# A 3x3 convolution with residual: the weights' load moved to third place on SyncE's queue, and other waits and semaphores for the loads

## The chip, the cores and the metric

The kernel runs on one core of a Trainium2 chip. The metric is the device time of one execution in microseconds (us); for the kernel before it is the median of three runs. A profile is one more execution, recorded by the hardware profiler, with its own span and time.

## The reference

Sixteen images with 64 channels of 64 x 64 pixels are convolved with a 3 x 3 kernel (64 channels out, zero padding of 1), and a residual is added, all in fp32:

```python
x:        (16, 64, 64, 64)      # batch, c_in, h, w
weight:   (64, 64, 3, 3)        # c_out, c_in, kh, kw
residual: (16, 64, 64, 64)
output[b, co] += weight[co, ci, kh, kw] * x_pad[b, ci, kh:kh+h, kw:kw+w]   # over ci, kh, kw
return output + residual
```

## The kernel before, in words

**Data and tiles.** Two images make a pair: 2 x 64 channels on 128 partitions, 4096 pixels each, 2 MB of fp32. There are eight pairs. Pair p of x is loaded into `xr[p % 3]`, one of three buffers. Its residual is loaded into `ro[p]`, one of eight; the sum is written in place there, and `ro[p]` is stored. So every pair costs three transfers of 2 MB. The weights (64 x 576 fp32, 144 KB) are loaded into `wdup`, which lies inside the last residual buffer, `ro[7]`.

**ScalarE** issues the weights' load (L125) and then packs the images. For each image n two copies (L135, L136) cast the even and the odd rows of x to bf16 and put them on the two halves of the partitions of `xp[n % 4]`. The first copy of a pair waits for the pair's load (`s_x`, L132), and from image 4 on each image waits until the convolution that last read its `xp` buffer is done (`s_conv`, L134).

**TensorE** first transposes the weights (L174), nine small matmuls into PSUM, as soon as DVE has doubled them (L145). Then it runs 16 convolutions of 24 matmuls each (L82 loads new weights first, L83 doesn't). Before an image it waits for a free PSUM half (`s_bank`, L178) and for the packed image (`s_pack`, L179). At the end of an image it raises `s_conv`. The result goes to `ps[n % 2]`, one of two halves of PSUM.

**DVE** clears the borders, waits for the weights (`s_w`, L144), doubles them (L145), casts the transposed weights to the bf16 tile `wl` (L152), and then adds the residual: for each image two adds (L163), for the even and the odd rows. It waits for the pair's residual (`s_r`, L160) and for the convolution (`s_conv`, L161). The first add of an image raises `s_add`, the second one frees the PSUM half (`s_bank`); of the last image both raise `s_add`.

**SyncE** issues all other transfers, in an order written out by hand: x0, r0, x1, r1, x2, r2, then for p = 3 to 7 a wait for the convolution of both images of pair p - 3 (L102), because pair p takes its x buffer, followed by x and r of that pair. The last residual also waits until the weights in its buffer have been transposed (`s_wt`). Then come the stores of pairs 0 to 4, each of which waits for `s_add` at 2p + 3 (L108), the first add of the next pair. The last three stores (L197) stand outside the critical section: they are issued when all engines have come to its end.

```python
        for p in range(NPAIR):
            if p >= NXR:
                nc.sync.wait_ge(s_conv, 2 * (p - NXR) + 2)
            load_x(p)
            if p == NPAIR - 1:
                nc.sync.wait_ge(s_wt, 2)
            load_ro(p)
        for p in range(NEARLY):
            nc.sync.wait_ge(s_add, 2 * p + 3)
            store(p).then_inc(s_out, 16)
```

Of the kernel before, what the change touches and what calls it, by code (L numbers as in the profile page):

```python
# [13 lines left out]
@with_exitstack  # L14
def kernel(
    ctx: ExitStack,
    tc: tile.TileContext,
    x: bass.AP,
    weight: bass.AP,
    residual: bass.AP,  # L20
    out: bass.AP,
):
    nc = tc.nc

    B, C, H, W = x.shape
    CO = weight.shape[0]
    K = weight.shape[2]
    assert C == 64 and CO == 64 and K == 3 and H == 64 and W == 64 and B == 16

    NPIX = H * W  # L30
    NPAIR = B // 2
    J = H // 2
    JC = 8
    NCHUNK = J // JC
    NXR = 3
    NXP = 4
    NEARLY = 5

    res_bc = residual.rearrange("b c h w -> (b c) (h w)")
    out_bc = out.rearrange("b c h w -> (b c) (h w)")  # L40
    x_bc = x.rearrange("b c h w -> (b c) (h w)")
    w_flat = weight.rearrange("co ci kh kw -> co (ci kh kw)")

    pool = ctx.enter_context(tc.tile_pool(name="pool", bufs=1))
    psum = ctx.enter_context(tc.tile_pool(name="psum", bufs=1, space=bass.MemoryType.PSUM))

    ident = pool.tile([64, 64], FP32)
    ro = [pool.tile([128, NPIX], FP32, name=f"ro{p}") for p in range(NPAIR)]
    xr = [pool.tile([128, NPIX], FP32, name=f"xr{i}") for i in range(NXR)]

    xp = [pool.tile([128, J + 1, W], BF16, name=f"xp{i}") for i in range(NXP)]

    wdup = ro[NPAIR - 1][0:64, 0:1152].rearrange("p (d f) -> p d f", d=2)
    wl = pool.tile([128, 2, 3, 2, 64], BF16)
    ps = [psum.tile([128, NCHUNK, JC, W], FP32, name=f"ps{i}") for i in range(2)]

    sem = lambda name: tc.alloc_semaphore(name)
    s_w = sem("s_w")
    s_x = [sem(f"s_x{p}") for p in range(NPAIR)]
    s_r = [sem(f"s_r{p}") for p in range(NPAIR)]  # L60
    s_out = sem("s_out")
    s_id = sem("s_id")
    s_wt = sem("s_wt")
    s_pack = sem("s_pack")
    s_bank = sem("s_bank")
    s_conv = sem("s_conv")
    s_add = sem("s_add")

    def load_x(p):
        nc.sync.dma_start(out=xr[p % NXR][:, :], in_=x_bc[128 * p : 128 * p + 128, :]).then_inc(s_x[p], 16)  # L70

    def load_ro(p):
        nc.sync.dma_start(out=ro[p][:, :], in_=res_bc[128 * p : 128 * p + 128, :]).then_inc(s_r[p], 16)

    def store(p):
        return nc.sync.dma_start(out=out_bc[128 * p : 128 * p + 128, :], in_=ro[p][:, :])

    def matmul(out_, lhsT, rhs, start, stop, ldweights):

        e = nc.tensor  # L80
        if ldweights:
            return e.matmul(out=out_, lhsT=lhsT, rhs=rhs, start=start, stop=stop, skip_group_check=True)  # L82
        return e.add_instruction(  # L83
            mybir.InstMatmult(
                name=nc.get_next_instruction_name(),
                engine=PE,
                ins=[e.lower_ap(rhs), e.lower_ap(lhsT)],
                outs=[e.lower_ap(out_)],
                start_tensor_calc=start,
                stop_tensor_calc=stop,  # L90
                tile_size=(128, 128),
                tile_position=(0, 0),
                bass_skip_group_check=True,
                ldweights=False,
            )
        )

    with tc.tile_critical(no_gpsimd_drain=True):  # L98

        for p in range(NPAIR):  # L100
            if p >= NXR:
                nc.sync.wait_ge(s_conv, 2 * (p - NXR) + 2)  # L102
            load_x(p)
            if p == NPAIR - 1:
                nc.sync.wait_ge(s_wt, 2)
            load_ro(p)
        for p in range(NEARLY):
            nc.sync.wait_ge(s_add, 2 * p + 3)  # L108
            store(p).then_inc(s_out, 16)


        nc.gpsimd.memset(ident[:, :], 0.0).then_inc(s_id, 1)  # L112
        nc.gpsimd.wait_ge(s_id, 1)
        nc.gpsimd.affine_select(  # L114
            out=ident[:, :],
            in_=ident[:, :],
            compare_op=mybir.AluOpType.not_equal,
            fill=1.0,
            base=0,
            pattern=[[-1, 64]],  # L120
            channel_multiplier=1,
        ).then_inc(s_id, 1)


        nc.scalar.dma_start(out=wdup[:, 0, :], in_=w_flat[:, :]).then_inc(s_w, 16)  # L125
        for n in range(B):
            p, im = divmod(n, 2)
            hp = slice(64 * im, 64 * im + 64)
            x4 = xr[p % NXR].rearrange("q (j two w) -> q j two w", two=2, w=W)
            t = xp[n % NXP]  # L130
            if im == 0:
                nc.scalar.wait_ge(s_x[p], 16)  # L132
            if n >= NXP:
                nc.scalar.wait_ge(s_conv, n - NXP + 1)  # L134
            nc.scalar.copy(out=t[64:128, 0:J, :], in_=x4[hp, :, 0, :])  # L135
            nc.scalar.copy(out=t[0:64, 1 : J + 1, :], in_=x4[hp, :, 1, :]).then_inc(s_pack, 1)  # L136


        for t in xp:
            nc.vector.memset(t[0:64, 0, :], 0.0)  # L140
            nc.vector.memset(t[64:128, J, :], 0.0)  # L141
        nc.vector.memset(wl[0:64, 0, :, 1, :], 0.0)  # L142
        nc.vector.memset(wl[64:128, 1, :, 0, :], 0.0)  # L143
        nc.vector.wait_ge(s_w, 16)  # L144
        nc.vector.tensor_copy(out=wdup[:, 1, :], in_=wdup[:, 0, :]).then_inc(s_wt, 1)  # L145
        nc.vector.wait_ge(s_wt, 2)
        tpf = ps[0].rearrange("p c j w -> p (c j) w")

        blocks = ((0, 0, 0, 0), (1, 0, 0, 1), (1, 0, 1, 0), (0, 1, 0, 2), (0, 1, 1, 1), (1, 1, 1, 2))
        for half, d, par, kh in blocks:  # L150
            hp = slice(64 * half, 64 * half + 64)
            i = nc.vector.tensor_copy(out=wl[hp, d, :, par, :], in_=tpf[hp, 3 * kh : 3 * kh + 3, :])  # L152
        i.then_inc(s_bank, 2)
        for n in range(B):
            p, im = divmod(n, 2)
            hp = slice(64 * im, 64 * im + 64)
            o4 = ro[p].rearrange("q (j two w) -> q j two w", two=2, w=W)
            psj = ps[n % 2].rearrange("q c j w -> q (c j) w")
            if im == 0:
                nc.vector.wait_ge(s_r[p], 16)  # L160
            nc.vector.wait_ge(s_conv, n + 1)  # L161
            for par in range(2):
                i = nc.vector.tensor_tensor(  # L163
                    out=o4[hp, :, par, :], in0=psj[64 * par : 64 * par + 64, :, :], in1=o4[hp, :, par, :], op=ADD
                )

                i.then_inc(s_add if par == 0 or n == B - 1 else s_bank, 1)


        nc.tensor.wait_ge(s_id, 2)  # L170
        nc.tensor.wait_ge(s_wt, 1)
        wdup3 = wdup.rearrange("p d (ci t) -> p (d ci) t", t=9)
        for t in range(9):
            i = nc.tensor.transpose(out=ps[0][:, t // 8, t % 8, :], in_=wdup3[:, :, t], identity=ident[:, :])  # L174
        i.then_inc(s_wt, 1)
        with nc.Fori(0, B // NXP, 1, engines=[PE]):
            for n in range(NXP):
                nc.tensor.wait_ge(s_bank, 1).then_inc(s_bank, -1)  # L178
                nc.tensor.wait_ge(s_pack, 1).then_inc(s_pack, -1)  # L179
                order = [(1, 0), (1, 1), (0, 0), (0, 1), (2, 0), (2, 1)]  # L180
                for i, (kw, d) in enumerate(order):
                    xlo, xhi = max(0, 1 - kw), min(W, W + 1 - kw)
                    for c in range(NCHUNK):
                        j0 = JC * c
                        m = matmul(
                            ps[n % 2][:, c, :, xlo:xhi],
                            wl[:, d, kw, :, :].rearrange("q r c -> q (r c)"),
                            xp[n][:, j0 + d : j0 + d + JC, xlo + kw - 1 : xhi + kw - 1],
                            i == 0,
                            i == len(order) - 1,  # L190
                            c == 0,
                        )
                m.then_inc(s_conv, 1)


    for p in range(NEARLY, NPAIR):
        store(p)  # L197
    with tc.tile_critical(sync_engine=mybir.EngineType.Pool, no_gpsimd_drain=True):
        nc.gpsimd.wait_ge(s_out, 16 * NEARLY)
# [30 lines left out]
```

## Time and profile before

| what | value |
|---|---|
| median of 3 runs | 124.96 us (124.82 to 125.03) |
| the profiled execution: its time | 125.16 us |
| the profiled execution: its span | 123.3 us |
| moved by DMA | 50.48 MB, mean 409 GB/s |
| TensorE matmuls, busy | 85.9 us (70% of the span) |
| VectorE (DVE), busy | 76.6 us (62%) |
| ScalarE (ACT), busy | 62.0 us (50%) |
| the adds, L163 | 32 of 2289 ns |
| the packing copies, L135 and L136 | 32 of about 1.9 us |

The span runs from the first to the last event that the profile shows of the program; the time is 1.9 us longer. Names in the profile: PE is TensorE's matmuls, PEld its weight loads, SP is SyncE, and SPq or ACTq is the queue of instructions on which SyncE or ScalarE issues transfers. In a row of the timeline stand the start and the duration in us, the engine, the line, the operation with the tile that it writes and the tile that it reads, and in brackets how long the engine had been idle and what ended that. A row of windows has the stretch, its length, the busy time of PE, PEld, DVE, ACT and POOL, PE's granted clock, the mean busy share of the 16 DMA engines and the GB/s. A row of waits has the total, the number of waits and the longest one. The weights are part of the buffer `ro`, and are shown under that name.

### The profile page before, as it was taken

The numbers are of one execution on the slowest core, as the hardware profiler recorded it, in microseconds if no ns is written. First come the engines' busy times: TensorE is split into PE (matmuls) and PEld (weight loads), VectorE is DVE, ScalarE is ACT, GpSimd is POOL, SyncE is SP. The second block draws the span as 40 slices with busy tenths as digits, with TensorE's granted clock in tenths as the row PEclk, the third lists the DMA queues.
The fourth block names the chain that finished last, engine by engine and source line by source line (L and its number), as shares of the span: only waits on it lengthen the run. The fifth ranks groups of instructions, "written<-read, shape, count | busy, mean of one in ns | idle before, by whom it ended". The sixth has DMA issues, their size and how long they took to land.

```text
span 123.3 us, 730 instructions
## 1 busy us (share of the span) xinstructions
PE 85.9 (70%) x389; PEld 10.6 (9%) x105; DVE 76.6 (62%) x49; ACT 62.0 (50%) x33; POOL 0.6 (0%) x6
## 2 busy tenths in 40 slices
PE   0004499999999999999999999999999900000000
PEld 0003001010101111010111101011110000000000
DVE  3003301989789798798978979889897895000000
ACT  4007966984993993993994796698000000000000
POOL 1000000000000000000000000000000000000000
PEclk9999999999999999999999999999999996555555
DMA  4999999999999999999999999999999999999992
GB/s 90 378 360 430 425 425 430 430 430 436 430 430 425 430 430 425 436 430 425 425 425 425 430 425 425 425 425 436 436 430 436 441 430 425 436 430 425 425 430 85
DMA packets 3536, 50.48 MB, mean 409 GB/s; under 512 B 400, under 2 KB 400, under 8 KB 464
## 3 DMA queue, kind: packets, MB, share of 16 engines
q1 hardware_dynamic: 3456, 50.33, 96.8%
q10 hardware_dynamic: 80, 0.15, 0.3%
HBM read 33.70 MB, written 16.78 MB: 409 GB/s over the span
## 4 chain that ended last, share of the span: by engine, by line
PE 69%; DVEq 2%; DVE 2%; issue 0%
PE ps L83 52%; PE ps L82 17%; DVEq L98 2%; DVE ro L163 2%
## 5 line engine op out<-in xcount | busy, mean ns | idle before, releaser
L163 DVE TENSOR_TENSOR ro<-ps,ro 64x2048 f32<-64x2048 f32 x32 | 73.2, 2289 | 16.6 <-PE ps L83 16.1
L83 PE MATMUL ps<-xp,wl 128*128 128x504 bf16 (+1 forms) x288 | 79.3, 385 | 0.2
L135 ACT CAST xp<-xr 64x2048 bf16<-64x2048 f32 x16 | 30.3, 1896 | 22.3 <-DMA xr<-in_x_dram 22.1
L82 PE MATMUL ps<-xp,wl 128*128 128x504 bf16 (+1 forms) x92 | 35.5, 385 | 2.4 <-PEq L179 2.4
L136 ACT CAST xp<-xr 64x2048 bf16<-64x2048 f32 x16 | 30.4, 1897 | 0.2
L82 PEld LDWEIGHTS ps<-xp,wl 128*128 128x128 bf16 x96 | 9.5, 99 | 76.8 <-issue 76.8
L174 PE MATMUL ps<-ident,ro 64*128 64x64 f32 x9 | 1.3, 320 | 10.3 <-DVE ro L145 10.3
L145 DVE COPY ro<-ro 64x576 f32<-64x576 f32 x1 | 0.5, 452 | 7.3 <-DMA ro<-in_weight_dram 7.3
L152 DVE CAST wl<-ps 64x192 bf16<-64x192 f32 x6 | 2.0, 352 | 1.5 <-PE ps L174 1.4
L135 ACT ACT_TABLE_LOAD x1 | 1.3, 1283 | 1.5 <-SPq L98 1.5
L174 PEld LDWEIGHTS ps<-ident,ro 64*128 64x128 f32 x9 | 1.1, 205 | 10.3 <-issue 10.3
L140 DVE MEMSET xp<- 64x32 uint32 x4 | 0.3, 85 | 1.2 <-SPq L98 1.0
L141 DVE MEMSET xp<- 64x32 uint32 x4 | 0.3, 85 | 0.2
L114 POOL TENSOR_SCALAR_AFFINE_SELECT ident<-ident 64x64 f32<-64x64 f32 x1 | 0.2, 233 | 0.2 <-POOL ident L112 0.2
L143 DVE MEMSET wl<- 64x96 uint32 x1 | 0.1, 138 | 0.1
L142 DVE MEMSET wl<- 64x96 uint32 x1 | 0.1, 138 | 0.1
L112 POOL MEMSET ident<- 64x64 f32 x1 | 0.1, 145 | 0.5 <-SPq L98 0.5
L214 POOL MEMSET const-bfloat16-1.0<- 128x1 bf16 x1 | 0.1, 107 | 0.0
L214 POOL MEMSET const-uint8-127<- 128x1 uint8 x1 | 0.1, 107 | 0.0
L214 POOL MEMSET const-float32-0.0<- 128x1 f32 x1 | 0.1, 104 | 0.2 <-issue 0.2
L214 POOL MEMSET const-float32-1.0<- 128x1 f32 x1 | 0.1, 104 | 0.0
## 6 DMA issues: line engine op xcount, KB each, us to landing
xr<-in_x_dram SPq DMA_DIRECT2D x8, 2048.0 KB, 12.0
ro<-in_residual_dram SPq DMA_DIRECT2D x8, 2048.0 KB, 16.5
out_dram<-ro SPq DMA_DIRECT2D x8, 2048.0 KB, 21.6
ro<-in_weight_dram ACTq DMA_DIRECT2D x1, 144.0 KB, 8.8
```

The lines of the kernel that those rows point to most:

```text
L82: return e.matmul(out=out_, lhsT=lhsT, rhs=rhs, start=start, stop=stop, skip_group_check=True)
L83: return e.add_instruction(mybir.InstMatmult(name=nc.get_next_instruction_name(), engine=PE, ins=[e.lower_ap(rhs), e.lower_ap(lhsT)], outs ...
L98: with tc.tile_critical(no_gpsimd_drain=True):
L135: nc.scalar.copy(out=t[64:128, 0:J, :], in_=x4[hp, :, 0, :])
L136: nc.scalar.copy(out=t[0:64, 1 : J + 1, :], in_=x4[hp, :, 1, :]).then_inc(s_pack, 1)
L140: nc.vector.memset(t[0:64, 0, :], 0.0)
L141: nc.vector.memset(t[64:128, J, :], 0.0)
L145: nc.vector.tensor_copy(out=wdup[:, 1, :], in_=wdup[:, 0, :]).then_inc(s_wt, 1)
L152: i = nc.vector.tensor_copy(out=wl[hp, d, :, par, :], in_=tpf[hp, 3 * kh : 3 * kh + 3, :])
L163: i = nc.vector.tensor_tensor(out=o4[hp, :, par, :], in0=psj[64 * par : 64 * par + 64, :, :], in1=o4[hp, :, par, :], op=ADD)
L174: i = nc.tensor.transpose(out=ps[0][:, t // 8, t % 8, :], in_=wdup3[:, :, t], identity=ident[:, :])
L214: nc = _bacc.Bacc("TRN2", target_bir_lowering=False, num_devices=1)
```

## The change

The weights are no longer loaded by ScalarE. SyncE loads them, behind x0 and r0 and ahead of x1. The loads of x3 to x7 wait for `s_add` where they waited for `s_conv`, with the same number: for the first add of the pair's second image instead of that image's last matmul. The eight semaphores for x and the eight for the residual become three each, with thresholds of 16, 32 and 48 as they are used again. On ScalarE and DVE the wait for `s_conv` is attached to the copy or add itself and no longer an instruction of its own; on DVE it stands behind the wait for the residual as before.

```diff
-    s_x = [sem(f"s_x{p}") for p in range(NPAIR)]
-    s_r = [sem(f"s_r{p}") for p in range(NPAIR)]
+    s_x = [sem(f"s_x{i}") for i in range(NXR)]
+    s_r = [sem(f"s_r{i}") for i in range(NXR)]
...
     def load_x(p):
-        ....then_inc(s_x[p], 16)
+        ....then_inc(s_x[p % NXR], 16)
     def load_ro(p):
-        ....then_inc(s_r[p], 16)
+        ....then_inc(s_r[p % NXR], 16)
...
         for p in range(NPAIR):
             if p >= NXR:
-                nc.sync.wait_ge(s_conv, 2 * (p - NXR) + 2)
+                nc.sync.wait_ge(s_add, 2 * (p - NXR) + 2)
             load_x(p)
             if p == NPAIR - 1:
                 nc.sync.wait_ge(s_wt, 2)
             load_ro(p)
+            if p == 0:
+                nc.sync.dma_start(out=wdup[:, 0, :], in_=w_flat[:, :]).then_inc(s_w, 16)
...
-        nc.scalar.dma_start(out=wdup[:, 0, :], in_=w_flat[:, :]).then_inc(s_w, 16)
         for n in range(B):
...
             if im == 0:
-                nc.scalar.wait_ge(s_x[p], 16)
+                nc.scalar.wait_ge(s_x[p % NXR], 16 * (p // NXR + 1))
+            i = nc.scalar.copy(out=t[64:128, 0:J, :], in_=x4[hp, :, 0, :])
             if n >= NXP:
-                nc.scalar.wait_ge(s_conv, n - NXP + 1)
-            nc.scalar.copy(out=t[64:128, 0:J, :], in_=x4[hp, :, 0, :])
+                i._wait_ge(s_conv, n - NXP + 1)
             nc.scalar.copy(out=t[0:64, 1 : J + 1, :], in_=x4[hp, :, 1, :]).then_inc(s_pack, 1)
...
             if im == 0:
-                nc.vector.wait_ge(s_r[p], 16)
-            nc.vector.wait_ge(s_conv, n + 1)
+                nc.vector.wait_ge(s_r[p % NXR], 16 * (p // NXR + 1))
             for par in range(2):
                 i = nc.vector.tensor_tensor(
...
+                if par == 0:
+                    i._wait_ge(s_conv, n + 1)
```

## The prediction

> **What bounds the kernel now.** I began with the slices of the span, because they show which resource is never idle.
>
> ```profile
> PE   0004499999999999999999999999999900000000
> DMA  4999999999999999999999999999999999999992
> GB/s 90 378 360 430 425 425 430 430 430 436 430 430 425 430 430 425 436 430 425 425 425 425 430 425 425 425 425 436 436 430 436 441 430 425 436 430 425 425 430 85
> ```
>
> One slice is 3.08 us. TensorE stops after slice 32 (98.8 us); the DMA engines are full from slice 2 to slice 39. 50.48 MB at 430 GB/s is 117.4 us of a 123.3 us span, so the transfers set the time. The chain of waits names PE for 69% of the span, but it ends with the last add at 103.4 us; the last 20 us are stores, which it does not show. A delay of PE therefore costs time only if it lets the DMA queue run dry, and the question is how much queued work there is ahead of each issue. The SyncE waits and its timeline say when it issues:
>
> ```profile
> SPq L70 <- PE ps L83: 60.4, 5, 22.2
> ...
> 26.21 0.33 SPq L70 DMA_DIRECT2D xr<-in_x_dram  x1
> ...
> 67.70 0.33 SPq L70 DMA_DIRECT2D xr<-in_x_dram  x1
> ...
> 103.73 1.58 SPq L76 DMA_DIRECT2D out_dram<-ro  x3
> ```
>
> Five x loads (pairs 3 to 7) wait for PE; the first of them goes out at 26.21, the last at 67.70, each 10.37 us after the one before. The last three stores follow the last add at 103.73. When each load lands is seen in the timelines, because ScalarE starts a pair's first cast as its x lands:
>
> ```profile
> 9.86 1.90 ACT L135 CAST xp<-xr 64x2048 bf16<-64x2048 f32 x1 [7.10 <-DMA xr<-in_x_dram]
> ...
> 19.51 1.90 ACT L135 CAST xp<-xr 64x2048 bf16<-64x2048 f32 x1 [2.02 <-DMA xr<-in_x_dram]
> ...
> 78.25 1.90 ACT L135 CAST xp<-xr 64x2048 bf16<-64x2048 f32 x1 [2.16 <-DMA xr<-in_x_dram]
> ```
>
> From x1 on, pairs land every 9.79 us ((78.25 - 19.51) / 6), 4.89 us per 2 MB transfer. So r0 lands at about 19.51 - 4.89 = 14.6, r2 at 34.2, r6 at 73.4, r7 at 83.1, and eight stores end at 83.1 + 39.1 = 122.2, 1.1 us before the span's end. The queue's cover, counted to a landing, is 34.2 - 26.2 = 8.0 us at the issue of x3 and shrinks by 0.58 (10.37 - 9.79) a pair to 73.4 - 67.7 = 5.7 us at x7. The last stores have 107.6 - 103.7 = 3.9 us. The start of PE:
>
> ```profile
> 9.69 0.45 DVE L145 COPY ro<-ro 64x576 f32<-64x576 f32 x1 [7.28 <-DMA ro<-in_weight_dram]
> ...
> 10.29 1.26 PE L174 MATMUL ps<-ident,ro 64*128 64x64 f32 x9 [10.29 <-DVE ro L145]
> 11.58 2.00 DVE L152 CAST wl<-ps 64x192 bf16<-64x192 f32 x6 [1.44 <-PE ps L174]
> ...
> 13.93 0.59 PE L82 MATMUL ps<-xp,wl 128*128 128x512 bf16 x1 [2.38 <-PEq L179]
> ```
>
> Weights land at 9.69, are transposed and cast by 13.58, and PE starts at 13.93, released by the first image's packing (done at 13.67). Both arrive together now.
>
> [...]the 0.15 MB of weights, alone on ScalarE's row, needed 8.8 us because they shared the engines with x0. On SyncE's row they will be served after r0. [...]here nothing moves until 1.5 us after the span's start for an issue at 0.95. [...]the first eight matmuls here take 3.37 us (13.93 to 17.30), the next eight 1.73. That start-up moves along with the start and is not paid anew.
>
> **The change, part by part.**
>
> 1. Weights third on SyncE's queue. Before, they shared the stream with x0:
>
> ```profile
> 3.10:6.20 3.10, 0.00 (x0) 0.00 (x0) 0.00 (x0) 0.00 (x0) 0.00 (x0) 1.00 0.94 383
> 6.20:9.30 3.10, 0.00 (x0) 0.00 (x0) 0.00 (x0) 0.00 (x0) 0.00 (x0) 1.00 0.99 357
> 9.30:34.00 24.70, 21.28 (x93) 3.36 (x31) 14.06 (x13) 19.83 (x11) 0.00 (x0) 1.00 1.01 430
> ```
>
> The last column is GB/s. From 6.2 to 9.3 it is 357 against 430: 73 x 3.1 / 430 = 0.53 us lost, which I put down to the mixing, and the weights' own bytes are 0.147 / 0.430 = 0.34 us. So x0 and r0 each land 0.87 us earlier: r0 at 13.7. The weights then pass in about 0.4 us (an estimate from the 0.34) and land at 14.1, 4.4 us later than 9.69. Bounds: 13.6 (they overlap r0's tail) to 15.1 (no gain for r0, 0.5 us of their own). Copy, transposes and casts keep their 3.89 us, so wl is ready at 13.58 + 4.4 = 17.98; the packing is then long done. With 0.15 us of handover (the copy ends at 10.14, PE starts at 10.29) PE starts at 18.1: **shift S = 4.2 us** (3.7 to 5.2). All of PE, DVE and the image-paced ScalarE casts shift by S. The stream as a whole is 0.5 us shorter. SyncE issues one more DMA (0.54 us on ScalarE's queue) ahead of x1 to r2; they stand in a queue that is full until about 33.7, so that costs nothing. Its cover is gone only if the queue ran dry before x1, which r0's 4.9 us excludes.
>
> 2. The x loads wait for the first add of the pair's second image instead of its last matmul. That add takes 2.29 us (the row of L163) and starts within 0.02 us of the convolution's end (67.71 against the issue at 67.70). So x3 to x7 go out 2.3 us later, besides S. Behind each stands its residual load, behind the last also stores 0 to 4; store 4 needs the first add of image 10, 72.97 + 2.29 + 4.2 = 79.5, later than the 74.2 below but under cover of five transfers. The rest waits for nothing new.
>
> 3. Semaphores and attached waits: the instruction listings of both kernels show every copy and add with the same wait on the same instruction as before (wait_ge was already merged into the next one), only with other semaphores and thresholds. Cost zero; anything that they might still add or save per image on DVE lies inside the 0.5 us that DVE idles before each image. Three counters are safe for time: pair p+3 is issued only after pair p was consumed, so no wait is released early or late.
>
> **The sum.** The last load decides. x7 goes out at 67.70 + 2.3 + 4.2 = 74.2. A load into an empty queue lands 8.0 us after issue: x0 took 8.9, less the 0.87 of the weights. If its descriptors arrive while the engines still finish r6, part of the start-up is hidden; it consists of some 0.8 us to the first byte and 1.0 us of slow ramp (0.54 MB by 4.0 us in half-microsecond windows, as if full rate had begun at 2.74). Without the ramp 7.0 us. So x7 lands at 81.2 to 82.2 instead of 78.25: 3.0 to 3.9 us late. Check forward from the first gap: x3 goes out at 26.21 + 6.5 = 32.7 and lands at 39.7 to 40.7 against 38.6 (34.2 - 0.5 + 4.9), a first loss of 1.1 to 2.1; then the queue, faster than PE by 0.58 a pair, gives that much for each of the next four at most: 3.4 to 4.4, less the 0.5 saved, the same result. After x7, r7 and eight stores follow without a gap: 122.2 + 3.0 to 3.9. A second route says the same: the last stores go out at 103.73 + 4.2 = 107.9; store 4 lands at 107.6 + 3.5 = 111.1, so their cover is 3.2 us, with 8.0 - 4.9 = 3.1 needed. So even if the x loads kept their old wait, S alone would cost 107.9 + 8.0 + 2 x 4.9 - 122.2 = 3.5 us (2.5 without the ramp).
>
> I take the middle, +3.5 us: 125.16 becomes 128.7 for the profiled execution (span 126.8); the median of the runs was 124.96, 0.2 lower, so 128.5 is the forecast.
>
> **Rivals.**
> - *Late weights* (0.15): the small rows (2304 bytes each, "under 8 KB" in the page) go slowly or r0 does not gain, S = 5.2. Then 129.5; with the full ramp 129.9. For it: that the weights took 8.8 us; against it: that this is explained by sharing.
> - *Cheap refill or early weights* (0.12): S of 3.7 and a slow ramp that belongs to the kernel's first load alone: 124.96 + 2.5 = 127.5; with only 6.5 us from issue to landing 127.0. Against it: the only refill that the trace has, x0, needed the longer time.
> - *Faster* (0.04): the weights are not held behind r0[...] and land by 10.4 us. Deciding point: x7's natural landing is 77.75, and 67.70 + 2.3 + S + 7.0 stays under that for S below 0.7. Then only the mixing is saved: 124.4. Against it: x0 to x2 land at even spacing, in issue order.
> - *The cover holds* (0.04): S is of 1 us and the effects cancel, 125.0. And that the attached waits and the semaphores do nothing is already in the sum.
>
> **How the numbers follow.** The main case has 0.65 (128.0 to 128.9). Range 126.9 to 130.0: it takes in the late and cheap cases and leaves about 0.15 outside, mostly below. A measurement of this kernel can tell about 0.2% (0.25 us) from no change. Slower 0.92, same 0.04, faster 0.04.
>
> **What would show it.** Right: the copy of the weights starts near 14.1 and PE's first convolution near 18.1; SyncE's L70 waits end on DVE's add, at 32.7 and then every 10.37 us to 74.2; slices with fewer GB/s near 33 us, and small dips each 10.4 us until about 76; PE as dense as before. Wrong: weights landing near 10; a steady 430 GB/s throughout; the x loads waiting with more than 8 us of queue left; or PE itself stalling on s_pack in mid-kernel, which the sum excludes (x3 at 40.7 is packed by 44.5, image 6 starts at 51).

## The result, and the profile after

The changed kernel takes **132.12 us** (median of 6 runs, 131.93 to 132.95) against 124.91 us for the kernel before (6 runs): a ratio of **1.0589, 95% interval 1.0559 to 1.0619**, 7.2 us slower. The direction was forecast, the size was not: 128.5 us, at most 130.0. The profiled execution took 132.71 us with a span of 130.9 us. Comparisons leave out runs more than 1.5% above the fastest of their kernel; for three kernels below that hides a scatter, and their whole range is given there.

The slices of the changed kernel (3.27 us each), first TensorE, then the busy share of the DMA engines and GB/s:

```profile
PE   0000229999999999999999999999999900000000
DMA  4999999999589999989999999999999999999991
GB/s 100 386 431 414 342 446 416 431 441 421 145 350 446 421 350 401 451 305 386 431 335 365 441 371 345 441 376 431 441 421 436 436 431 436 421 436 436 421 441 60
```

The even row of 430 is gone. One slice falls to 145 (33 to 36 us), and until slice 27 some slice of every few stays between 305 and 401. PE is as dense as before, only later. Its start, from the timeline of the changed kernel:

```profile
15.04 0.45 DVE L147 COPY ro<-ro 64x576 f32<-64x576 f32 x1 [12.63 <-DMA ro<-in_weight_dram]
...
19.28 0.58 PE L82 MATMUL ps<-xp,wl 128*128 128x512 bf16 x1 [2.38 <-PEq L182]
...
22.65 0.63 PE L82 MATMUL ps<-xp,wl 128*128 128x504 bf16 x1
23.07 1.01 PE L83 MATMUL ps<-xp,wl 128*128 128x504 bf16 x3
23.92 0.38 PE L82 MATMUL ps<-xp,wl 128*128 128x504 bf16 x1
```

The weights land at 15.04 instead of 9.69, and PE starts 5.35 us later (19.28 against 13.93). Ten matmuls run at the slow pace this time (0.43 us from one start to the next, then 0.22), and the first twelve take 4.64 us, to 23.92; before, eight were slow, and the first twelve took 4.30. SyncE's issues of x3 and x7, and its waits (total, times, longest):

```profile
34.22 0.33 SPq L70 DMA_DIRECT2D xr<-in_x_dram  x1
...
75.71 0.33 SPq L70 DMA_DIRECT2D xr<-in_x_dram  x1
```

```profile
SPq L70 <- DVE ro L164: 67.8, 5, 29.6
```

x3 and x7 go out 8.01 us later than before (26.21 and 67.70), and the releaser is now the add. Where the loads land is seen again from ScalarE's first cast of each pair:

```profile
29.59 1.90 ACT L135 CAST xp<-xr 64x2048 bf16<-64x2048 f32 x1 [2.22 <-DMA xr<-in_x_dram]
...
41.89 1.90 ACT L135 CAST xp<-xr 64x2048 bf16<-64x2048 f32 x1 [4.67 <-DMA xr<-in_x_dram]
...
53.02 1.90 ACT L135 CAST xp<-xr 64x2048 bf16<-64x2048 f32 x1 [3.49 <-DMA xr<-in_x_dram]
...
65.04 1.90 ACT L135 CAST xp<-xr 64x2048 bf16<-64x2048 f32 x1 [4.39 <-DMA xr<-in_x_dram]
...
75.41 1.90 ACT L135 CAST xp<-xr 64x2048 bf16<-64x2048 f32 x1 [2.73 <-DMA xr<-in_x_dram]
...
85.85 1.90 ACT L135 CAST xp<-xr 64x2048 bf16<-64x2048 f32 x1 [2.80 <-DMA xr<-in_x_dram]
```

A full queue would put 9.79 us between them, as from x1 on in the kernel before. There are 12.30, 11.13, 12.02, 10.37 and 10.44: losses of 2.51, 1.34, 2.23, 0.58 and 0.65 us, **7.3 us together**. The stores behind them follow without a gap. So nearly the whole time went in the loads x3 to x7. The first loss in windows of 1 us (the last column is GB/s):

```profile
33.00:34.00 1.00, 1.00 (x6) 0.10 (x1) 1.00 (x1) 0.97 (x2) 0.00 (x0) 1.00 0.12 49
34.00:35.00 1.00, 1.00 (x7) 0.15 (x2) 0.97 (x2) 1.00 (x1) 0.00 (x0) 1.00 0.00 0
35.00:36.00 1.00, 1.00 (x6) 0.14 (x2) 1.00 (x1) 0.99 (x2) 0.00 (x0) 1.00 1.42 262
```

By the times of their single packets (16 KB each, 0.61 us), the engines run out of r2's data between 33.1 and 33.9, and none takes up x3, issued at 34.22, before 35.17.

### The profile page after: what moved, and what is told of

It reads as the page before. It is cut to its first block, busy times and chain, and to the rows that moved or that the text cites. A ratio compares the mean times of both kernels' runs of the same rounds, so it can differ in the third digit from the quotient of the medians.

```text
span 130.9 us, 730 instructions
## 1 busy us (share of the span) xinstructions
PE 86.3 (66%) x389; PEld 10.6 (8%) x105; DVE 76.6 (59%) x49; ACT 62.0 (47%) x33; POOL 0.6 (0%) x6
## 2 busy tenths in 40 slices
DMA packets 3536, 50.48 MB, mean 386 GB/s; under 512 B 400, under 2 KB 400, under 8 KB 464
## 3 DMA queue, kind: packets, MB, share of 16 engines
q1 hardware_dynamic: 3536, 50.48, 94.6%
## 4 chain that ended last, share of the span: by engine, by line
PE 65%; DVEq 2%; DVE 2%; issue 0%
PE ps L83 49%; PE ps L82 16%; DVEq L98 2%; DVE ro L164 2%
```

## The experiments

The landings of a single transfer are read from the trace: it has 16 of them for each, which are taken here as one for each of the 16 DMA engines, and a transfer counts as landed with the last of them. **Cover** is the time from the issue of a load or store to the last landing of the transfer ahead of it. Covers and losses come from the one profiled execution of each kernel.

**Which part of the change costs?** First the weights' place alone (`w_only`):

```diff
+            if p == 0:
+                nc.sync.dma_start(out=wdup[:, 0, :], in_=w_flat[:, :]).then_inc(s_w, 16)
...
-        nc.scalar.dma_start(out=wdup[:, 0, :], in_=w_flat[:, :]).then_inc(s_w, 16)
```

> The weights third on SyncE's queue, everything else as before (x loads wait for the last matmul, eight semaphores each). Theory A, late weights alone empty the queue: PE starts near 19.3 as in the kernel after, x7 is issued near 73.4 (67.70 + 5.7), and by the loads or by the last stores (109.4 + 8 + 9.8) the end comes about 5 us late: 129 to 130.3 us. Rival B, both delays are needed (the cover of 5.7 us bears S but not S plus the add's 2.3 us): at most 126.5 us. Rival C, the add gate does it: 125.0 us.

Measured: 130.26 us, ratio 1.0403 (1.0374 to 1.0432). x7 was issued at 73.39 and landed at 82.70, 4.5 us later than before:

```profile
82.70 1.90 ACT L136 CAST xp<-xr 64x2048 bf16<-64x2048 f32 x1 [2.53 <-DMA xr<-in_x_dram]
```

So the late weights alone cost 4.0 of the 5.9%. Rivals B and C fall. The stores did not add to it: at the issue of store 5 some 2.4 us were queued, and it landed 4.87 us after store 4, without loss.

The other parts alone: the changed kernel with the weights back on ScalarE's queue (`after_w_act`), and the kernel before with only the gate changed (`gate_only`):

```diff
-                nc.sync.wait_ge(s_conv, 2 * (p - NXR) + 2)
+                nc.sync.wait_ge(s_add, 2 * (p - NXR) + 2)
```

> The kernel after with the weights issued by ScalarE again, so only the gate on the add, the three semaphores and the attached waits are left of the change. Theory A: x7 is issued near 70.0, 3.3 us ahead of the landing of r6, and the time is that of before, 124.7 to 125.3 us. Rival C, a load issued after a wait on the add takes 10.1 us to land whatever the queue holds, as x5 to x7 did in the kernel after: x7 lands at 80.1 instead of 78.25 and the time is 126.8 us or more.

> The kernel before with the x loads waiting for the first add and nothing else changed (eight semaphores each, weights on ScalarE's queue). x7 is issued near 70.0 with 3.3 us of queue left to the landing of r6. If the scatter of the kernel after with the weights back on ScalarE (124.9 to 128.6 us) comes from this thin cover: the same scatter here, lowest runs at 124.9, several above 126.5 us. If it comes from the three semaphores or the attached waits: 124.7 to 125.5 us in all runs.

Measured: the 20 runs of `after_w_act` go from 124.87 to 128.62 us. Ten of them reach at most 125.37 us and come to 0.9993 of the kernel before (0.9977 to 1.0009); the other ten lie above 126.8. `gate_only` ran at 124.74, 126.33, 127.23 and 127.23. So the gate alone can be free, and in half of the runs or more it costs 1.3 to 3.6 us. The scatter is there with the gate alone, so the semaphores and attached waits are not needed for it, and the ten lower runs of `after_w_act` show that they cost nothing. In both profiles x7 (cover 3.1 and 3.3 us) landed without loss, and what was lost (0.4 and 1.3 us) was lost in r7, behind it; what sets that loss is open (last section). On top of the late weights the other parts cost 1.9 us (132.1 against 130.3). The three residual semaphores without the gate on the add were not tried: nothing in the program would then keep r3 from raising r0's counter before DVE's wait for r0 has passed.

**The place or the queue?** The changed kernel, and the kernel before, with the weights first on SyncE's queue:

```diff
+        nc.sync.dma_start(out=wdup[:, 0, :], in_=w_flat[:, :]).then_inc(s_w, 16)
         for p in range(NPAIR):
             if p >= NXR:
```

> The kernel after with the weights first on SyncE's queue, ahead of x0, so that it differs from the kernel after by the place in the queue alone. Theory A: the weights land before 5, PE is released by the first image's packing near 14 and the time is 124.5 to 125.2 us. If the queue that carries the weights matters, and not their place in it, it stays above 128 us.

> The kernel before with the weights first on SyncE's queue and nothing else changed. [...]if mixing two rows cost 0.5 us, 124.4 us; if the weights cost the stream the same 0.9 us wherever they stand, 124.9 us. x0 lands near 9.6 either way.

> The weights first on SyncE's queue, otherwise the kernel before, with more rounds for a narrower interval: 0.9979 of the kernel before, as measured, 124.7 us.

Measured: the nine runs of `after_w_first` go from 124.61 to 128.54 us, with the scatter of the gate; the five lowest, up to 126.09, come to 1.0006 (0.9971 to 1.0041). All nine lie below the 131.9 of the changed kernel's fastest run: the place decides, not the queue. `w_first` came to 0.9979 (0.9967 to 0.9991) and, repeated, 0.9995 (0.9983 to 1.0007): at most 0.2%, and not told from nothing in the second series. So taking the weights out of the mixture with x0 saves next to nothing. One reason is in the traces of both: behind the weights x0 is issued at 1.57 us instead of 0.95.

**Is it the empty queue, or PE's late end?** `w_only` with an earlier gate: ScalarE's first copy of the next pair raises a new semaphore, and x3 to x7 wait for that; two more stores are issued inside the section.

```diff
-    NEARLY = 5
+    NEARLY = 7
...
-                nc.sync.wait_ge(s_conv, 2 * (p - NXR) + 2)
+                nc.sync.wait_ge(s_xf, p - NXR + 1)
...
+            if im == 0 and n > 0:
+                i.then_inc(s_xf, 1)
```

> The weights still third on SyncE's queue, so PE starts near 19.3 as in the kernel after; but the x loads wait only until their buffer has been packed by ScalarE (a new semaphore raised by the next pair's first copy), which is 10 us earlier or more, and the stores of pairs 5 and 6 are issued inside the critical section. Theory A, the late weights cost time only through an empty queue: with more than 10 us of queued work at each issue the time goes back to 124.6 to 125.3 us, though PE ends 5.7 us later than before. Rival D, the late start of PE itself costs (PE or the last add sets the end): 129 us or more as with the old waits.

Measured: 125.56 us, ratio 1.0051 (1.0034 to 1.0069). Its slices, and its last adds behind those of the kernel before:

```profile
GB/s 96 377 435 430 356 435 430 425 425 430 430 430 425 425 435 425 430 425 425 425 425 425 425 435 430 435 425 451 425 425 435 430 435 430 425 425 425 435 435 69
```

```profile
98.83 4.61 DVE L163 TENSOR_TENSOR ro<-ps,ro 64x2048 f32<-64x2048 f32 x2 [0.51 <-PE ps L83]
```

```profile
104.33 4.61 DVE L167 TENSOR_TENSOR ro<-ps,ro 64x2048 f32<-64x2048 f32 x2 [0.51 <-PE ps L84]
```

The weights are as late as in `w_only` (their copy starts at 14.68) and the last adds start and end 5.5 us later than in the kernel before, but the row is even again and 4.7 us of the 5.2 are back. **The late weights cost through the empty queue**; rival D falls. The last store landed at 121.91, earlier than the 122.17 of the kernel before, so the 0.6 us that the medians leave is not in the transfers of this execution; where it lies is open.

**What does one thin cover cost?** The kernel before with a single x load held back, all others as they were:

```diff
-                nc.sync.wait_ge(s_conv, 2 * (p - NXR) + 2)
+                nc.sync.wait_ge(s_conv, 2 * (p - NXR) + 2 + (1 if p == 5 else 0))
```

(`x5_conv_next`; p == 3 and p == 4 in `x3_conv_next` and `x4_conv_next`; `x5_add_next` waits for `s_add` at the same number, `x7_add` for `s_add` without the extra 1.)

> The kernel before; only x5 waits for one convolution more (image 6 instead of 5). It is issued near 52.2, 1.6 us ahead of the landing of r4 at 53.75, and would land at 58.64 without loss. Theory A (a load that finds less than some 3 us of queue loses time on each engine, most on the slowest): it lands at 59.3 to 60.8, time 125.7 to 127.1 us. The prediction's own model (it lands 7.0 us after issue or without loss): 59.2, 125.5 us.

> The kernel before; only x5 waits for the first add of image 6. It is issued near 54.5, 0.75 us behind the landing of r4, into an empty queue. This measures the refill: with 7.6 us from issue to landing, as x3 in the kernel after, it lands at 62.1 and the time is 128.4 us; with 7.0 us 61.5 and 127.8 us; with 10.1 us, as x5 to x7 there, 64.6 and 130.9 us.

> The kernel before; only x3 waits for one convolution more. It is issued near 31.5: 2.7 us ahead of the last of r2's 16 landings (34.18), 1.8 us ahead of the first (33.31). Theory A (any of the 16 engines that has less than 2.2 to 2.5 us of work at the issue loses time): x3 lands 0.5 to 1.5 us later than 39.08, the landings of the 16 engines spread by more than 1 us, and the time is 125.5 to 126.5 us. The prediction's own model (landing 7.0 us after issue, or without loss): 39.08, no loss, 125.0 us.

> The kernel before; only x7 waits for the add. Its cover is the thinnest of the kernel whose x loads all wait for the add: 3.3 us to the last landing of r6, 2.5 us to the first. If the scatter of that kernel comes from this one load at the edge: the same scatter, some runs at 124.9 and some above 126 us, with the loss at x7 or r7. If it needs all five loads to be late: 124.7 to 125.4 us.

> The kernel before; only x4 waits for one convolution more. It is issued near 41.8, 2.1 us ahead of the last of r3's 16 landings and 1.3 us ahead of the first. The prediction's formula (landing 7.8 us after issue, or without loss) gives x4 a loss of 0.8 us (49.6 instead of 48.86), time 125.7 us. If the slowest of the 16 engines pays the whole restart as soon as its own work is short, while the median engine follows the formula: last landing 50.4 to 51, median landing loss 0.5 us, time 126.5 to 127.2 us.

The refill of an empty queue, from `x5_add_next` (issue of x5 on SyncE, first cast of x5 on ScalarE):

```profile
54.76 0.33 SPq L70 DMA_DIRECT2D xr<-in_x_dram  x1
```

```profile
62.57 1.90 ACT L135 CAST xp<-xr 64x2048 bf16<-64x2048 f32 x1 [6.21 <-DMA xr<-in_x_dram]
```

From issue to landing 7.8 us, of which 4.89 are the transfer. The trace's packets show where some of the rest goes: the first one starts 0.95 us after the issue, and the first sixteen take 0.8 to 1.8 us each, against 0.61 later on (x3 in the changed kernel: 0.95 us, and 0.96 to 1.84). If 7.8 us is the least from issue to landing, a load that finds a cover below 7.8 - 4.89 = 2.9 us should lose the difference. The table holds that against the first disturbed load of each kernel, with the engines still in step (loss: last landing less that of the transfer ahead, less 4.89):

| load | cover | 2.9 - cover | measured loss | time |
|---|---|---|---|---|
| x3 in `x3_conv_next` | 2.89 | 0.0 | 0.2 | 125.99, 1.0081 (1.0055 to 1.0107) |
| x7 in `x7_add` | 2.80 | 0.1 | 0.3 | 127.52, 1.0192 (1.0138 to 1.0246) |
| x3 in `w_only` | 2.20 | 0.7 | 2.0 (the median engine 0.5) | 130.26 |
| x4 in `x4_conv_next` | 1.71 | 1.2 | 1.0 | 126.79, 1.0147 (1.0108 to 1.0185) |
| x5 in `x5_conv_next` | 0.42 | 2.5 | 2.5 | 127.92, 1.0219 (1.0182 to 1.0257) |
| x3 in the changed kernel | 0.17 | 2.7 | 2.5 | 132.12 |
| x5 in `x5_add_next` | -1.17 | 4.1 | 4.1 | 129.78, 1.0379 (1.0337 to 1.0422) |

The last row fits by construction, as the 2.9 was taken from it. Of the other six, five lie within about 0.2 us of the line, and so does x3 in `late_x67_early` below (cover -0.6, 3.5 on the line, 3.3 measured). My expectation that the slowest engine always pays a whole restart failed at `x3_conv_next` and `x4_conv_next` and holds only for x3 in `w_only`. x5 in `x5_conv_next` had less cover than planned because PE's start-up was slower in that execution (DVE idled 8.70 us before its first add, waiting for the first convolution, against 7.52 in the kernel before). The times of the five kernels with one load held back contain a second loss, of 0.5 to 1.6 us, in r7 (last section). All four runs of `x7_add` lie above 126.3 us, so one late load at the end is enough for slow runs. It does not explain the scatter of the gate: none of the four came near 124.9, and in the profile 1.6 us were lost in r7 and only 0.3 in x7.

**Why do x5 to x7 go on losing?** In the changed kernel they had covers of 2.9, 4.5 and 4.5 us. But the engines are no longer in step there: r2's 16 landings spread over 0.8 us, x4's over 1.8, x5's over 2.8, x6's over 2.3. `late_x67_early` takes the thin cover away from x6 and x7 only:

```diff
+                if p < 6:
+                    nc.sync.wait_ge(s_add, 2 * (p - NXR) + 2)
+                else:
+                    nc.sync.wait_ge(s_xf, p - NXR + 1)
```

> Weights third, x3 to x5 wait for the add as in the kernel after, but x6 and x7 only for the packing of their buffer, so that they are issued with much work queued while the 16 engines are already out of step; eight semaphores each. If the loss needs thin cover at each issue: x3 to x5 lose as in the kernel after (x5 lands near 65), x6 and x7 follow without loss (74.7 and 84.5), time 130.5 to 131.2 us. If engines out of step keep losing by themselves: x7 lands near 85.8 and the time is that of the kernel after, 132 us.

Measured: 131.43 us, ratio 1.0514 (1.0473 to 1.0556). x3, x4 and x5 lost 3.3, 1.5 and 0.5 us; x6 and x7 then landed without loss, 9.78 us apart by ScalarE's first casts, though the spread stayed at 1.5 us:

```profile
74.04 1.90 ACT L140 CAST xp<-xr 64x2048 bf16<-64x2048 f32 x1 [2.13 <-DMA xr<-in_x_dram]
...
83.82 1.90 ACT L140 CAST xp<-xr 64x2048 bf16<-64x2048 f32 x1 [2.14 <-DMA xr<-in_x_dram]
```

So engines out of step lose nothing by themselves; a short cover has to come to it. That the cover of the first engine to finish is the one that counts is a reading that fits in part. Counted to the first engine's landing the covers of x5, x6 and x7 in the changed kernel were 1.0, 1.7 and 2.2 us, and the line gives 1.9, 1.2 and 0.7 against 2.2, 0.6 and 0.7 measured. For x4 to x7 in `w_only` it gives 1.5, 1.5, 1.2 and 0.7, and measured were 0.5, 1.0, 0.5 and 0.4: right in kind, up to three times too large. The packets also show what these losses are made of. Averaged over the 16 engines, in the changed kernel the engines stood idle for 0.2 to 0.5 us around each of x4 to x7, and single packets that took up to 2.4 us instead of 0.61 cost a further 0.5 to 0.9 us. At x3 the idle time was the larger part (about 1.8 us, and 0.9 in slow packets). So the later losses came more from slow packets than from idle engines; why the packets become slow is open. The trace does not name the engine of a landing, so whether the same engine stays behind is open.

**A version for use.** Weights first and the early gate together (`w_first_pack5`):

> A version for use: the weights first on SyncE's queue, and the x loads gated by the packing of their buffer instead of the convolution, so that more than 10 us of work is queued at each issue; five early stores as before. Nothing in the kernel before runs dry, so more cover brings nothing: as with the weights first alone, 124.6 to 124.9 us, 0.2% under the kernel before. If thin cover costs the kernel before something after all, 124.3 us or less.

Measured: 124.81 us, ratio 0.9989 (0.9978 to 0.9999). It is ahead of both kernels, but of the kernel before by 0.1% only, which is no more than a measurement can tell. The stream of 50.48 MB is the bound, and from x1 to x7, 9.79 us apart in the kernel before, there was no idle time in it that more cover could win.

## Why the prediction was wrong

- **What bounds the kernel** held: PE's lateness is free while the queue is full (`w_only_pack`: last adds 5.5 us later, time 0.6 us longer), and the loss arises at the issues of x3 to x7. The direction and the parts that cost nothing held, too.
- **The shift S was 5.35 us, not 4.2.** The step that failed: "x0 and r0 each land 0.87 us earlier: r0 at 13.7". x0 did (8.75, last landing, against 9.84), but r0 landed at 14.30 instead of 14.59 and the weights 0.7 us behind it. From 12 to 15 us the changed kernel moved only

```profile
12.00:13.00 1.00, 0.00 (x0) 0.00 (x0) 0.00 (x0) 0.98 (x2) 0.00 (x0) 1.00 0.92 362
13.00:14.00 1.00, 0.00 (x0) 0.00 (x0) 0.00 (x0) 1.00 (x1) 0.00 (x0) 1.00 1.38 310
14.00:15.00 1.00, 0.00 (x0) 0.00 (x0) 0.00 (x0) 0.99 (x2) 0.00 (x0) 1.00 0.76 295
```

  GB/s: (68 + 120 + 135) / 430 = 0.75 us short. Landings agree: x1 came 10.96 us behind x0, where two transfers and the weights' bytes take 9.79 + 0.34, so 0.8 us were lost. So the weights cost the stream no less behind r0 than beside x0, and x1 landed at 19.71 instead of 19.49, not 0.5 us earlier. The weights' own rows took 0.09 us each in both kernels (median); behind r0, 23 large packets beside them took 0.7 to 1.2 us instead of 0.61. My late bound of 15.1 was the true case, and I gave it 0.15.
- **"That start-up moves along with the start and is not paid anew"** failed by 0.34 us (4.64 against 4.30 for the first twelve): two more slow matmuls. (A reading was off as well: before, the eight matmuls behind the slow eight took 1.80 us, 17.30 to 19.10, not 1.73, which is the pace after that.) The start-up differs from one profile to the next: DVE idled 7.52 us before its first add in the kernel before, 7.78 in the changed kernel, 7.91 in `x5_add_next` and 8.70 in `x5_conv_next`. And x3, where its wait was left alone and the weights on ScalarE, was issued at 26.21, 26.44, 26.66, 26.67 and 27.65 in the five kernels, the last one in `x5_conv_next`. What sets the number of slow matmuls was not shown. With the add's 2.3 us, x7 was issued 8.0 us late instead of 6.5.
- **The refill** was 7.8 us, near the upper end of my 7.0 to 8.0. That the slow ramp might hide while the queue runs out is what the table speaks against: x4 in `x4_conv_next` and x7 in `x7_add` were issued while the queue still ran, and from issue to landing they needed 7.6 and 8.0 us, about as long as a load into an empty queue.
- **The step that failed most** is "the queue, faster than PE by 0.58 a pair, gives that much for each of the next four at most". It treats the 16 engines as one queue that loses only the time in which it is empty. Measured were 1.34, 2.23, 0.58 and 0.65 us, 4.8 instead of at most 2.3.
- **The sum** for x7's landing (7.6 us late by the cast, 78.25 to 85.85): 3.5 forecast, 1.5 from the later issue, 0.3 from the refill against the middle of my range, and 2.3 left for engines out of step. The last is a remainder: `late_x67_early` shows that the part of x6 and x7 goes away when they have cover, and the single packets show that the later losses are mostly slow packets; the size is not derived.
- **The second route**, that the last stores alone would cost 3.5 us, assumed that with the old wait the x loads lose nothing, so that store 4 lands at 107.6. By its own figures x7 would then have 5.7 - 4.2 = 1.5 us of cover, where 3.1 are needed. In `w_only` the loads lost first, store 4 landed at 111.84, and store 5 lost nothing with 2.4 us queued, where a load would have lost 0.5 on the line.
- Of the rivals, "late weights" named the right shift and still fell short of the time by 2.6 us (2.2 with the full ramp), as it kept the same refill and the same single queue.

## What to carry to other kernels

When transfers bound a kernel, compute for each issue how much queued work is ahead of it, and compare that with the time from issue to landing less the transfer itself (here 2.9 us); delays that add up past it were paid here, in full at the first load (2.5 us at x3 of the changed kernel) and with more at the next ones (4.8 us at x4 to x7). A margin just above it was not safe: with 3.1 to 3.3 us left at the last load, half of the runs of `after_w_act` and three of the four of `gate_only` were slower by 1.3 us or more. With 12.7 us (`w_only_pack`) nothing was lost. The margin is best won by gating a load on the true last use of its buffer (here the packing) instead of a later event. A small transfer that starts the compute chain belongs ahead of the large ones (`w_first`: 0.9979 and 0.9995 of the kernel before), or beside them on another queue as in the kernel before; behind x0 and r0 the weights landed at 15.0 us instead of 9.7.

## What the runs showed that was not expected

- A load with thin cover can put the 16 engines out of step: in the changed kernel the spread of one transfer's landings grew from 0.8 us (r2) to 2.8 us (x5), and at the end of the last store it was still 1.8 us. In the kernel before it is 0.8 to 1.2 us throughout. It does not always happen: behind x4 in `x4_conv_next` (cover 1.71) the spread stayed at 0.7 us.
- In most kernels with a disturbed or thinly covered load, r7, the last load ahead of the stores, lost 0.4 to 1.6 us, also where everything between had been even: in `x3_conv_next` x3 lost 0.2 us at 39 us, nothing more was lost until x7 landed at 78.4, then r7 lost 0.75. No engine stood idle there: of r7's packets that started from 80 to 82 us, 22 took 0.8 to 1.2 us instead of 0.61. The kernel before and `w_only_pack` have none of these slow packets; `w_only` has 16 at this place, without a loss at the last landing. No run here settles the cause.
